# Margins on the estimated readiness of small products, and masked keys made one group ahead, in a two-layer decoder step

## The chip, the cores and the metric

The kernel runs on one core of a Trainium2 chip. The metric is the device time of one execution in microseconds (us). The core has five engines that the text names: PE (TensorE, the matrix products), DVE (VectorE), ACT (ScalarE), POOL (GpSimd) and SP (SyncE, which issues the DMA transfers). Each works through its own instructions in the order of the program and waits at an instruction until the data of the others are there.

## The reference

One inference step of a two-layer decoder of width 1024, for a prompt of 1024 tokens and for 8 samples of 4 new tokens each. Layer 0 is sliding-window attention with sinks, layer 1 is a gated DeltaNet. All data are float32. Cut to what matters:

```python
for layer in range(2):
    h = rms_norm(x, norm_g) * (1 + scale) + shift          # shift, scale, gate from silu(c) @ w_mod
    if layer == 0:                                         # 16 heads of 64, 4 kv heads, window 128
        q, k, v, z = split(h @ w_in)
        attn = sink_softmax(q k^T / 8, band) v             # samples: 128 cached keys and 4 new ones
        out = (attn * silu(z)) @ w_out
    else:                                                  # 8 key heads, 16 value heads of 128
        qkv, z, a, b = split(h @ w_in)
        q, k, v = silu(conv4(qkv))                         # depthwise, 4 taps; q, k normalized
        beta = sigmoid(b);  g = -exp(a_log) * softplus(a + dt_bias)
        for each chunk of 64 tokens:                       # w_v, w_k from a triangular solve
            u = w_v - w_k S
            o = (q e^gc) S + tril(q k^T decay) u
            S = S * e^(sum g) + (k e^(gtot - gc))^T u
        out = (rms_norm(o) * silu(z)) @ w_out
    x = x + gate * out
y = rms_norm(x, final_norm_g)
# outputs: y of prompt and samples, the new k/v caches, conv states and states S (8 x 16 x 128 x 128)
```

## The kernel before

**Products.** The large products are the four projections (in and out, of both layers). Each operand is split into a high and a low part of a shorter float format, and three products (high by high, high by low, low by high) are added up. In the profile they write `ps_pj`, `ps_tr` or `ps_ob` and read `hhi`/`hlo` or `h2hi`/`h2lo` with `wh`/`wl`; in the second out-projection the weights lie in `h2hi`, `h2lo`, `whB`, `wlB` and the moving side is `ohi`/`olo`. They depend on little and are the material with which PE is kept busy. Everything else on PE is small: transposes through the identity `cst`, products of single chunks or heads.

**How the order is made.** Each engine executes in program order, so the order in which the Python code emits instructions is all there is of a schedule. `Core` (L96 to L175) is a planner's clock: `issued` (L111) adds an estimated duration to `free[eng]` for each emitted instruction, from a table of rates (L130 to L144), and notes in `written` when each tile is ready. Every instruction passes the wrapper at L89, so nearly all rows of the profile say L89, and one goes by the names of tiles. The small steps are generators (the text calls them jobs) in a list sorted by rank (`weave` L485, ranks in `K` and `KR` at L241 and L242). After each large product `stages` (L496) goes through the list and lets each job run on while its condition is true. The conditions:

- `ready(*ts)` (L520): the tiles are estimated to be written by the time that PE's clock shows. It stands before a small product, so that the product is emitted when its operands should be there.
- `soon` (L523) and `idle` (L526): the same with 0.4 and 0.8 us of grace, before evacuations and work of other engines.
- `bank(tag)` and `give`: a PSUM bank of that tag (2 of `mi`, 2 of `lg`, 2 of `pj`, 1 of `tr`, 1 of `ob`).

Where no large product is to be had, `until` (L507) moves PE's clock on by 0.1 us and tries again; the emitted program then has no product in between, and PE really waits.

**The stages, in order of time** (from the trace). To 378 us the modulation and the projections and attention of layer 0. Then `cached` and `cached_pair` (L1034, L1067), the samples' attention: per pair of samples the keys `kc` are transposed, logits `ps_lg`, softmax into `sp` on DVE and ACT, `sp` transposed through `ps_mi` into `spT`, times the cached values `vc` into `ps_ob`. The z projection is the large work beside it. `gate_rows` (L423) then spreads the modulation over rows with a selection matrix `selt`. From 418 us the out-projection of layer 0, beside it `shape` (L1375), which scales and transposes blocks of the residual (`dg` is a diagonal of 1/rms) into the next layer's input.

From about 540 us layer 1. `decays` (L1501) makes the a/b projection `abT`, turns it into `AB`, from it the decays `g` and `gpr`, their running sum `gc` and the rows `gbs`; all that works with a chunk needs them. The heads go in eight pairs. For pair hq: `taps` (L1671) is the convolution on DVE from the projected rows `XR` into `qT`, `kT`, `vT` (`samples`, L1686, does it for the sample tokens, with the conv state `st`); `turn` in `proj_v` (L1734) transposes the values; `decay_blocks`, `solve`, `invert` and `blocks` make the triangular inverses (`X`, `UZ`, `us`, `DP`); `chain` (L1985) goes through the chunks in sequence with the state `S`, and `output` (L2031) is its product of queries, `uo` and state. The keys of pair r+1 are projected only when the chain of pair r-1 is finished (L2170).

From about 1455 us the out-projection of layer 1, `out_block` (L2312), with the samples beside it: `core` (L2424) makes their delta rule in sample layout (`KQT`, `qk`, `oH`; its `turned`, L2438, is a transpose of several tiles), and the block of the 32 sample rows waits for `core` (L2200). `new_states` (L2621) updates the 8 x 16 states: per group of two head pairs ACT masks the keys of one sample into `kb` (96 rows), per head pair PE multiplies `kb` by `U96` (`U` in the profile) into a bank of `mi`, and DVE adds two halves to the loaded state (`S1` in the code, `S` in the profile), which SP stores when its group of heads is full. The last steps are the final norm of the last block, `xt`, and its store.

## Time and profile before

| | |
|---|---|
| median of 3 runs | 1741.56 us (1740.1 to 1749.42) |
| the profiled execution | span 1740.3 us, 31813 instructions |
| busy: PE, DVE, ACT, POOL | 94%, 69%, 50%, 35% |
| busy of PE, 600 to 700 us and 700 to 800 us | 91.07 and 81.83 of 100 us |
| busy of PE, 1100 to 1200 us | 99.50 of 100 us |
| DMA, mean | 110 GB/s |

The profile comes from one execution. A row of the timeline has start, duration, engine, the line, the operation, the tile written and the tiles read, and in brackets the time that the engine stood idle before it and what ended that. A row of the waits has the engine with the tile it wrote, what it waited for, the sum in us, the number of waits and the longest. A row of a stretch has the stretch, its length, the busy time of PE, its weight loads, DVE, ACT and POOL (in brackets how many instructions), the granted clock of TensorE as a share of full speed, the DMA share and GB/s.

### The profile page before, as it was taken

The numbers are of one execution on the slowest core, as the hardware profiler recorded it, in microseconds if no ns is written. First come the engines' busy times: TensorE is split into PE (matmuls) and PEld (weight loads), VectorE is DVE, ScalarE is ACT, GpSimd is POOL, SyncE is SP. The second block draws the span as 40 slices with busy tenths as digits, with TensorE's granted clock in tenths as the row PEclk, the third lists the DMA queues.
The fourth block names the chain that finished last, engine by engine and source line by source line (L and its number), as shares of the span: only waits on it lengthen the run. The fifth ranks groups of instructions, "written<-read, shape, count | busy, mean of one in ns | idle before, by whom it ended". The sixth has DMA issues, their size and how long they took to land. (4 is left out here: it accounts for less than half of the span.)

```text
span 1740.3 us, 31813 instructions
## 1 busy us (share of the span) xinstructions
PE 1635.4 (94%) x10666; PEld 1436.2 (83%) x10666; DVE 1200.4 (69%) x3538; ACT 862.1 (50%) x2514; POOL 605.8 (35%) x1170
## 2 busy tenths in 40 slices
PE   6999999998999889789999999999999998989897
PEld 5988888986777789579999999899998996667685
DVE  4526775654565678876878789778788775367676
ACT  4625555543334555156554655654756654343332
POOL 2601111122122244344454544545345454333332
PEclk9999999999999999899999999999999999999998
DMA  9542121133233322222422323224232137854885
GB/s 328 154 130 73 50 62 53 48 99 107 89 133 91 88 65 63 61 66 68 117 58 75 96 57 105 70 76 111 52 112 61 45 91 223 232 180 153 252 251 163
DMA packets 281573, 191.77 MB, mean 110 GB/s; under 512 B 98362, under 2 KB 253882, under 8 KB 281379
## 3 DMA queue, kind: packets, MB, share of 16 engines
q1 hardware_dynamic: 281410, 189.75, 37.6%
q8 instruction: 84, 1.38, 0.3%
q14 instruction: 79, 0.64, 0.1%
HBM read 144.68 MB, written 47.04 MB: 110 GB/s over the span
## 5 line engine op out<-in xcount | busy, mean ns | idle before, releaser
L89 PE MATMUL ps_pj<-h2hi,wh 128*128 128x384 f32 (+1 forms) x1128 | 380.5, 337 | 2.1 <-ACT wh L89 2.1
L89 PE MATMUL ps_pj<-h2hi,wl 128*128 128x384 f32 (+1 forms) x1128 | 380.0, 337 | 0.7 <-POOL wl L89 0.7
L89 PE MATMUL ps_pj<-h2lo,wh 128*128 128x384 f32 (+1 forms) x1128 | 377.8, 335 | 0.0
L89 POOL TENSOR_TENSOR wl<-wr,wh 128x512 fp32r<-128x512 f32 x122 | 165.9, 1361 | 526.6 <-ACT wh L89 465.5
L89 PEld LDWEIGHTS ps_pj<-h2hi,wh 128*128 128x128 f32 x1128 | 214.1, 190 | 4.6 <-ACT wh L89 2.5
L89 PEld LDWEIGHTS ps_pj<-h2hi,wl 128*128 128x128 f32 x1128 | 214.2, 190 | 3.8 <-POOL wl L89 1.1
L89 PEld LDWEIGHTS ps_pj<-h2lo,wh 128*128 128x128 f32 x1128 | 213.9, 190 | 2.5
L89 POOL TENSOR_TENSOR xt<-xt,y 128x512 f32<-128x512 f32 (+1 forms) x48 | 64.0, 1338 | 173.8 <-DVE y L89 142.4
L89 DVE SCALAR_TENSOR_TENSOR vT<-XR,cT,vT 128x384 f32<-128x384 f32 (+1 forms) x144 | 95.3, 675 | 39.8 <-ACT vT L89 38.1
L89 PE MATMUL ps_pj<-hlo,wh 128*128 128x384 f32 (+1 forms) x360 | 119.0, 331 | 0.0
L89 PE MATMUL ps_pj<-hhi,wh 128*128 128x384 f32 (+1 forms) x360 | 118.4, 329 | 0.0
L89 PE MATMUL ps_pj<-hhi,wl 128*128 128x384 f32 (+1 forms) x360 | 117.9, 328 | 0.0
L89 DVE TENSOR_TENSOR tmp<-X 64x31 f32<-64x31 f32 (+15 forms) x248 | 93.7, 378 | 9.4 <-POOL X L89 5.9
L89 DVE TENSOR_TENSOR X<-X,tmp 64x31 f32<-64x31 f32 (+15 forms) x248 | 89.1, 359 | 8.5
L89 ACT CAST wh<-wr 128x512 fp32r<-128x512 f32 x122 | 75.2, 617 | 13.2 <-PE ps_pj L89 9.0
L89 PEld LDWEIGHTS ps_pj<-hlo,wh 128*128 128x128 f32 x360 | 67.7, 188 | 11.2 <-issue 11.1
L89 ACT ACTIVATE vo<-vo,fo 128x128 f32<-128x128 f32 x128 | 42.4, 392 | 61.5 <-POOL fo L89 61.5
L89 POOL TENSOR_TENSOR rst<-rsw 128x4 f32<-128x4 f32 x96 | 24.2, 252 | 131.8 <-DVE rsw L89 122.9
L89 PEld LDWEIGHTS ps_pj<-hhi,wh 128*128 128x128 f32 x360 | 67.7, 188 | 2.7 <-issue 2.7
L89 ACT COPY XR<-ps_pj 128x384 f32<-128x384 f32 (+1 forms) x96 | 43.0, 448 | 54.2 <-PE ps_pj L89 54.2
L89 ACT ACTIVATE prob<-prob,nm 128x256 f32<-128x256 f32 (+1 forms) x128 | 62.2, 489 | 14.8 <-DVE nm L89 14.6
L89 PEld LDWEIGHTS ps_pj<-hhi,wl 128*128 128x128 f32 x360 | 67.7, 188 | 2.1 <-issue 2.1
(580 smaller groups left out, 4262.0 us busy)
## 6 DMA issues: line engine op xcount, KB each, us to landing
wr<-in_gdn_w_in SPq DMA_DIRECT2D x96, 256.0 KB
S<-in_state_gdn_s SPq DMA_DIRECT2D x40, 256.0 KB
xt<-in_x_prompt SPq DMA_DIRECT2D x16, 512.0 KB
wm<-in_w_mod SPq DMA_DIRECT2D x16, 512.0 KB
wr<-in_swa_w_in SPq DMA_DIRECT2D x64, 128.0 KB
wmod<-in_w_mod SPq DMA_DIRECT2D x32, 256.0 KB
wm<-in_w_mod SPq DMA_DIRECT2D x32, 256.0 KB
DP<-gcr SPq DMA_DIRECT2D x64, 128.0 KB
```

The lines of the kernel that those rows point to most:

```text
L89: inst = fn(*args, **kwargs)
```

## The change

`ready` gets a margin, `lag`, in microseconds of the planner's clock: the product is emitted only when PE's clock is that much past the estimated readiness. At fifteen places a margin is given:

| place | tiles | margin |
|---|---|---|
| `gate_rows` L431 | `selt` | 2.5 |
| `cached_pair` L1079, L1112, L1122 | `kc`; `sp`; `pT` (`spT` in the profile) and `vc` | 1.5; 1.0; 1.0 |
| `shape` L1387 | `dg`, `xt` | 2.0 |
| `decays` L1536, L1583, L1590, L1621 | `abT`; `gp_` (`gpr`); `gc`; `gbs` | 1.5; 3.5; 1.0; 1.0 |
| `samples` L1687 | `st`, `XR` | 1.5 |
| `turn` L1736 | `u` (`vT` of the profile), `irk` | 1.0 |
| `output` L2035 | `S`, `uo` | 0.6 |
| `turned` L2438; for KQ L2544 | its sources (`qk`, `oH` and others); `KQT` | 1.0; 3.0 |
| `new_states` L2655 | `kb`, `U96`, `st` | 0.5 |

In `new_states` the mask `kb` of the next group is made behind the first product of a group, where before it was made in front of the product that reads it. There are two buffers of `kb` in both.

```diff
-    def ready(*ts):
-        return lambda: plain() or nc.ready(ts) <= nc.free["tensor"]
+    def ready(*ts, lag=0.0):
+        return lambda: plain() or nc.ready(ts) + lag <= nc.free["tensor"]
...
-        yield ready(gp_)
+        yield ready(gp_, lag=3.5)
...
+        def masked(g):
+            b, hq = g // 4, 2 * (g % 4)
+            kb = su.tile([96, 2, P], F32R, tag="kb", name="kb", bufs=2)
+            nc.scalar.activation(kb.rearrange("p h k -> p (h k)"), f(K96[:, hq * P:(hq + 2) * P]), AF.Copy,
+                                 scale=C["bsel"][0:96, b:b + 1])
+            return kb
+
+        g = 0
+        yield idle("scalar", K96)
+        ahead = masked(0)
         while units:
             fetch()
             b, h0, n, st = units.pop(0)
             for hh in range(n // 2):
                 hq = h0 // 2 + hh
                 if hh % 2 == 0:
-                    yield idle("scalar", K96)
-                    kb = su.tile([96, 2, P], F32R, tag="kb", name="kb", bufs=2)
-                    nc.scalar.activation(kb.rearrange("p h k -> p (h k)"), f(K96[:, hq * P:(hq + 2) * P]), AF.Copy,
-                                         scale=C["bsel"][0:96, b:b + 1])
-                yield ready(kb, U96, st)
+                    kb, g = ahead, g + 1
+                yield ready(kb, U96, st, lag=0.5)
                 pu = yield from bank("mi")
                 nc.tensor.matmul(pu[:, 0:256], kb[:, hh % 2, :], U96[:, 2 * hq * P:(2 * hq + 2) * P],
                                  start=True, stop=True)
+                if hh % 2 == 0 and g < 4 * DB:
+                    yield idle("scalar")
+                    ahead = masked(g)
```

No instruction is added or left out; the order moves on every engine from the samples' attention on, since each condition that comes true later moves all that follows it. Three places show it.

DVE in `decays`, between the a/b values and `gpr` (`pl` is a polynomial, `x` and `g` the decays; `qT` and `kT` are taps of the convolution of head pair 0, with the projected rows `XR`). Before:

```order
L89 SCALAR_TENSOR_TENSOR kT<-XR_5998,cT,kT 128x256
L89 SCALAR_TENSOR_TENSOR qT<-XR_5999,cT,qT 128x384
L89 SCALAR_TENSOR_TENSOR kT<-XR_5998,cT,kT 128x256
L89 SCALAR_TENSOR_TENSOR qT<-XR_5999,cT,qT 128x384
L89 SCALAR_TENSOR_TENSOR kT<-XR_5998,cT,kT 128x256
L89 SCALAR_TENSOR_TENSOR pl<-pl,s_6335 128x144 x7
L89 SCALAR_TENSOR_TENSOR pl<-pl,s 128x144
L89 SCALAR_TENSOR_TENSOR qT<-XR_5999,cT,qT 128x256
L89 TENSOR_SCALAR x<-x 128x144
L89 SCALAR_TENSOR_TENSOR x<-pl,x 128x144
L89 SCALAR_TENSOR_TENSOR g<-x,al 128x144
L89 COPY gpr<-g 128x128
```

and of the change:

```order
L89 TENSOR_SCALAR pl<-s_6363 128x144
L89 SCALAR_TENSOR_TENSOR kT<-XR_5943,cT,kT 128x256
L89 SCALAR_TENSOR_TENSOR pl<-pl,s_6363 128x144
L89 SCALAR_TENSOR_TENSOR kT<-XR_5943,cT,kT 128x256
L89 SCALAR_TENSOR_TENSOR pl<-pl,s_6363 128x144
L89 SCALAR_TENSOR_TENSOR kT<-XR_5943,cT,kT 128x256
L89 SCALAR_TENSOR_TENSOR pl<-pl,s_6363 128x144 x5
L89 SCALAR_TENSOR_TENSOR pl<-pl,s 128x144
L89 TENSOR_SCALAR x<-x 128x144
L89 SCALAR_TENSOR_TENSOR x<-pl,x 128x144
L89 SCALAR_TENSOR_TENSOR g<-x,al 128x144
L89 COPY gpr<-g 128x128
```

Before, four `qT` taps stand between `AB` and `gpr` (the first right in front of these rows); in the change none does, and the three `kT` taps stay.

PE in the second out-projection, at the transposes of `oH` in `core` and behind them. Before (the first `64x512` product, of the sample rows' block, comes 19 rows behind the first row):

```order
L89 MATMUL ps_lg<-cst,oH 128x128 x4
L89 MATMUL ps_mi<-U_17847,kb 128x256
L89 MATMUL ps_tr<-h2hi,ohi 128x512
L89 MATMUL ps_tr<-h2hi,olo 128x512
L89 MATMUL ps_tr<-h2lo,ohi 128x512
L89 MATMUL ps_ob<-h2hi,ohi 128x512
L89 MATMUL ps_ob<-h2hi,olo 128x512
L89 MATMUL ps_ob<-h2lo,ohi 128x512
L89 MATMUL ps_mi<-U_17847,kb 128x256
L89 MATMUL ps_ob<-h2hi,ohi 128x512
```

and of the change:

```order
L89 MATMUL ps_ob<-h2hi,ohi 128x512
L89 MATMUL ps_ob<-h2hi,olo 128x512
L89 MATMUL ps_ob<-h2lo,ohi 128x512
L89 MATMUL ps_lg<-cst,oH 128x128 x4
L89 MATMUL ps_mi<-U_17847,kb 128x256 x6
L89 MATMUL ps_pj<-h2hi,ohi 64x512
```

The out-projection's large products of this block have moved in front of `oH`; behind it stand six products of new states and then the sample block.

PE at the end of the program. Before:

```order
L89 MATMUL ps_ob<-h2lo,ohi 128x512
L89 MATMUL ps_ob<-h2hi,ohi 128x512
L89 MATMUL ps_ob<-h2hi,olo 128x512
L89 MATMUL ps_ob<-h2lo,ohi 128x512
L2712 UNCONDITIONAL_BRANCH
```

and of the change:

```order
L89 MATMUL ps_ob<-h2hi,ohi 128x512
L89 MATMUL ps_ob<-h2hi,olo 128x512
L89 MATMUL ps_ob<-h2lo,ohi 128x512
L89 MATMUL ps_mi<-U_17847,kb 128x256 x5
L2722 UNCONDITIONAL_BRANCH
```

Five products of new states, which before stood ahead of the last block, now stand behind the last product of the out-projection.

More of the change, by code (lines that the diff above doesn't have):

```diff
@@ L430, in gate_rows @@
         for j in range(2):
-            yield ready(selt)
+            yield ready(selt, lag=2.5)
             pg = yield from bank("lg")
@@ L1078, in cached_pair @@
             for r in range(2):
-                yield ready(kc)
+                yield ready(kc, lag=1.5)
                 pt = yield from bank("mi")
@@ L1111, in cached_pair @@
             nc.vector.tensor_scalar_mul(sp, sp, su)
-            yield ready(sp)
+            yield ready(sp, lag=1.0)
             pt = yield from bank("mi")
@@ L1121, in cached_pair @@
             give("mi", pt)
-            yield ready(pT, vc)
+            yield ready(pT, vc, lag=1.0)
             for kv in range(4):
@@ L1386, in shape @@
             for kk in range(2):
-                yield ready(dg, xt)
+                yield ready(dg, xt, lag=2.0)
                 pt = yield from bank("lg")
@@ L1535, in decays @@
             give("lg", pj)
-        yield ready(abT)
+        yield ready(abT, lag=1.5)
         pt = yield from bank("lg")
@@ L1589, in decays @@
         nc.vector.tensor_copy(gcf, pt[:, 0:P])
-        yield ready(gc)
+        yield ready(gc, lag=1.0)
         p2 = yield from bank("lg")
@@ L1620, in decays @@
         weave(decayed(0, states[0]), "decayed", 0)
-        yield ready(gbs)
+        yield ready(gbs, lag=1.0)
         pt = yield from bank("lg")
@@ L1686, in samples @@
                     def samples():
-                        yield ready(st, XR[:, TP:])
+                        yield ready(st, XR[:, TP:], lag=1.5)
                         pt = yield from bank("tr")
@@ L1735, in turn @@
                         yield lambda: "irk" in st
-                        yield ready(u, st["irk"])
+                        yield ready(u, st["irk"], lag=1.0)
                         pt = yield from bank("tr")
@@ L2034, in output @@
                 vt = vo[cp_]
-                yield ready(S, uo)
+                yield ready(S, uo, lag=0.6)
                 pb = psb("mi")
@@ L2436, in t2, with turned @@
             return sl.tile([P, DS, P], dt, tag="t2", name=nm, bufs=4)
-        def turned(dst, srcs, parts=P):
-            yield ready(*srcs)
+        def turned(dst, srcs, parts=P, lag=1.0):
+            yield ready(*srcs, lag=lag)
             pt = yield from bank("lg")
@@ L2544, in core @@
             yield from turned(lambda pt: nc.scalar.copy(KQ[:, (1 - i) * DS:(2 - i) * DS, :].rearrange("p t d -> p (t d)"), pt),
-                              [KQT[:, :, i, t] for t in range(DS)])
+                              [KQT[:, :, i, t] for t in range(DS)], lag=3.0)
         uH = VH
```

## The prediction

> **What bounds the kernel.** First the page, then the busy time by stretches of 100 us, for a full and a poor stretch.
>
> ```profile
> span 1740.3 us, 31813 instructions
> PE 1635.4 (94%) x10666; PEld 1436.2 (83%) x10666; DVE 1200.4 (69%) x3538; ACT 862.1 (50%) x2514; POOL 605.8 (35%) x1170
> ```
> ```profile
> 700.00:800.00 100.00, 81.83 (x600) 70.19 (x599) 76.22 (x215) 43.81 (x137) 34.97 (x99) 0.90 0.21 59
> 1100.00:1200.00 100.00, 99.50 (x705) 93.86 (x704) 79.33 (x230) 60.09 (x193) 45.27 (x115) 1.00 0.32 86
> ```
>
> TensorE (PE) is busy for 94% of the span. At 1100 us it has no time to give; at 700 us it is short by 18% and has a granted clock of 0.90. So time can only come from PE's waits and from the clock they cost. PE's waits, by what ended them (total, times, longest):
>
> ```profile
> PE ps_mi L89 <- ACT kb L89: 8.9, 3, 5.8
> PE ps_tr L89 <- ACT vT L89: 7.7, 3, 6.0
> PE ps_mi L89 <- ACT uo L89: 7.2, 4, 2.8
> PE ps_mi L89 <- DVE UZ L89: 6.6, 5, 2.1
> PE ps_lg L89 <- DVE KQT L89: 4.0, 1, 4.0
> PE ps_lg L89 <- DVE gpr L89: 3.2, 1, 3.2
> PE ps_tr L89 <- ACT XR L89: 2.6, 1, 2.6
> PE ps_lg L89 <- issue: 2.2, 1, 2.2
> PE ps_mi L89 <- DMA kc<-in_cache_swa_k: 2.2, 2, 1.1
> PE ps_lg L89 <- DVE dg L89: 2.0, 2, 1.7
> PE ps_ob L89 <- DVE spT L89: 1.4, 2, 0.8
> PE ps_mi L89 <- DVE sp L89: 1.2, 2, 0.6
> PE ps_tr L89 <- ACT vo L89: 2.4, 3, 1.4
> ```
>
> All but UZ and vo are places that get a margin: 8.9 + 7.7 + 7.2 + 4.0 + 3.2 + 2.6 + 2.2 + 2.2 + 2.0 + 1.4 + 1.2 = 42.6 us. Each is a small product at PE's head, in front of large products that were ready. A wait also costs clock: the last figure but two of each stretch is the granted clock, and around the one wait for XR a large product lengthens.
>
> ```profile
> 405.00:420.00 15.00, 10.78 (x111) 7.51 (x110) 5.70 (x27) 5.47 (x16) 0.00 (x0) 0.77 0.19 56
> 640.00:660.00 20.00, 13.95 (x83) 13.35 (x83) 14.43 (x32) 16.05 (x48) 7.83 (x13) 0.83 0.12 30
> 1555.00:1575.00 20.00, 15.96 (x68) 13.05 (x67) 18.33 (x45) 6.12 (x15) 7.38 (x5) 0.83 0.54 171
> 1615.00:1635.00 20.00, 14.19 (x54) 11.25 (x53) 10.84 (x25) 5.23 (x11) 4.92 (x4) 0.83 0.89 272
> ```
> ```profile
> 780.59 0.30 PE L89 MATMUL ps_tr<-cst,XR 128*35 128x128 f32 x1 [2.64 <-ACT XR L89]
> 781.08 0.34 PE L89 MATMUL ps_pj<-h2hi,wl 128*128 128x384 f32 x1
> 781.84 0.52 PE L89 MATMUL ps_pj<-h2hi,wl 128*128 128x384 f32 x1
> ```
>
> A clock of 0.83 over 20 us is 20 x 0.17 = 3.4 us of full-speed work lost. Behind a wait of only 2.64 us a product goes from 0.34 to 0.52 us. [...]
>
> **Part by part** (gains negative).
>
> *Cached attention, 378 to 420 us.* The margins of kc, sp and pT/vc eat their waits. But the last z products now stand one softmax earlier, and the last pair has none.
>
> ```profile
> 407.27 0.32 DVE L89 CUSTOM_DVE_ANT_0 sp<-ps_lg,smk 128x160 f32<-128x160 f32 x1
> ```
> ```profile
> 410.77 0.41 PE L89 MATMUL ps_mi<-cst,sp 128*128 128x128 f32 x2 [0.65 <-DVE sp L89]
> 415.38 1.19 PE L89 MATMUL ps_lg<-modG,selt 128*128 128x512 f32 x1 [2.21 <-issue]
> ```
>
> From the start of the last pair's softmax to the transpose of its weights it is 410.77 - 407.27 = 3.5 us; large products cover all of it but 0.65. Now only small ones stand there, of which I count two of 0.41, which leaves 2.7 bare, then 0.8 for spT. The selection (the product of 415.38; its wait is the row of 2.2 put down to issue) moves behind the first out-projection products, and its 2.2 goes over to these, whose operand comes out of the same last steps. Against 2.2 + 1.2 + 1.4 + 2.2 = 7.0 now, 2.7 + 0.8 + 2.2 = 5.7: **-1** (ends -7, nothing bare, and +3, if the bare stretch costs a further 3.4 of clock).
>
> *Shaping, dg.* A margin of 2.0 against waits of 1.7 and 0.3: **-1.5** (-2 to 0).
>
> *Decays, head pair 0 and its chain, 570 to 770 us.* On DVE four qT taps leave the path from AB to gpr.
>
> ```profile
> 577.36 0.62 DVE L89 SCALAR_TENSOR_TENSOR qT<-XR,cT,qT 128x384 f32<-128x384 f32 x1
> 578.30 0.64 DVE L89 SCALAR_TENSOR_TENSOR qT<-XR,cT,qT 128x384 f32<-128x384 f32 x1
> 579.26 1.65 DVE L89 SCALAR_TENSOR_TENSOR qT<-XR,cT,qT 128x384 f32<-128x384 f32 x1
> 584.00 1.48 DVE L89 SCALAR_TENSOR_TENSOR qT<-XR,cT,qT 128x256 f32<-128x256 f32 x1
> 586.37 0.23 DVE L89 COPY gpr<-g 128x128 f32<-128x128 f32 x1
> 648.02 0.62 DVE L89 SCALAR_TENSOR_TENSOR vT<-XR,cT,vT 128x384 f32<-128x384 f32 x1 [5.12 <-ACT vT L89]
> ```
> ```profile
> 641.53 0.23 ACT L89 ACTIVATE us<-us 128x32 f32<-128x32 f32 x1 [4.81 <-POOL us L89]
> ```
>
> They are 0.62 + 0.64 + 1.65 + 1.48 = 4.4 us, so gpr comes 4.4 earlier and PE's 3.2 there goes. Up to 641.53 ScalarE (ACT) waited 4.81 us for POOL's `us`, with four exponentials and vT queued behind it; PE waited 6.0 and DVE, inside the inverse of pair 0, 5.1. In the new order that `us` stands behind the exponentials. Both put chain 0 ahead by 4.4 + 5.1 = 9.5. What PE itself saves ahead of that counts no further: in the stretch from 700 us it has no large product left (pair 2's keys wait for chain 0) and stands for UZ, 6.6 us, without a margin. **-9.5** (ends -12.7, if gpr's 3.2 counts as well, and -3, if the margins of abT, gc, gbs and turn push the chain back).
>
> *XR at 778 us.* A margin of 1.5 against 2.6, and 1.5 for the products that went at 0.52 for 0.34 behind it, some eight: **-3** (-4.3, the whole wait and 1.7, to 0).
>
> *800 to 1450 us.* uo without its longest, 7.2 - 2.8 = 4.4, and vT without its longest, 1.7: 6.1 to be had; a margin of 0.6 on uo takes a part: **-4** (-6.1 to +3, as every unneeded margin also delays). *uo at 1500 us*, 0.6 of 2.8: **-1** (-2.8 to 0).
>
> *The samples' core, 1520 to 1600 us.* KQT's margin of 3.0 leaves 1.0 of the 4.0, so -3.0, and with so short a wait the clock's 3.4 goes. Against that, the large products that lay behind oH now lie ahead of it, and the last block's first product follows oH with six products of U96 and kb between. Each of these is followed by two updates of S on DVE:
>
> ```profile
> L89 DVE SCALAR_TENSOR_TENSOR S<-S,gtb,ps_mi x128: 328/342/351, 1588.3 to 1716.8; 128x128 f32<-128x128 f32 x128
> ```
>
> 6 x 2 x 0.342 = 4.1 us bare, which also covers the samples' path from oH to their operand. -3.0 - 3.4 + 4.1 = **-2.5** (-7.4 to +1).
>
> *New states, 1588 to 1740 us.* The mask kb stands in ACT's queue behind casts that wait for data.
>
> ```profile
> 1620.31 0.62 ACT L89 CAST h2hi<-wr 128x512 fp32r<-128x512 f32 x1 [3.62 <-DMA wr<-in_gdn_w_out]
> 1624.79 0.62 ACT L89 CAST ohi<-of 128x512 fp32r<-128x512 f32 x1 [3.86 <-DMA of<-gTd]
> 1625.32 0.90 ACT L89 ACTIVATE kb<-K,cst 96x256 fp32r<-96x256 f32 x2
> ```
>
> A group ahead, kb is done before these. [...] Of PE's 5.8, about 2 stays, because its next large products need h2hi's cast of 1620.31 and the low part made from it. 5.8 - 2.0 = 3.8, the other kb waits 8.9 - 5.8 = 3.1, and half of the clock's 3.4: 8.6, of which I take **-8** (-12.3 to -2, if h2hi holds PE all the same).
>
> *The end.* Now PE's last kb product is at 1714.67 and the last output leaves SP at 1736.74, behind y's scaling alone.
>
> ```profile
> 1714.67 0.41 PE L89 MATMUL ps_mi<-U,kb 96*128 96x256 f32 x1
> ```
> ```profile
> 1736.74 0.81 SPq L89 DMA_DIRECT2D out_y_p<-xt  x2
> ```
>
> In the new order the last five of them follow the last out-projection product, with their updates of S between and behind the steps of y, and one more store of S behind out_y_p on SP. Two pairs of updates ahead of y's first step, one between, one behind: 4 x 2 x 0.342 = 2.7, and 0.8 of SP's time: **+3.5** (0, if DVE's gaps there take them, to +8, if the store's landing is bare).
>
> *Fresh waits.* From 378 us on, most rows have moved against each other. Where no margin helps, such a wait is 0.8 us (vo: 2.4 in 3); ten of them, an estimate, **+8** (+4 to +12).
>
> Sum: -1 - 1.5 - 9.5 - 3 - 4 - 1 - 2.5 - 8 + 3.5 + 8 = **-19**. The profiled execution, span 1740.3, is 1.3 below the runs' median of 1741.56; it becomes 1721.3, the median **1722.5**. The margins add no instruction.
>
> **Rivals.**
>
> *All waits go.* If the bare stretches above are covered, 42.6 us of waits and the clock of the four stretches, 3 x 3.4 + 15 x 0.23 = 13.7, less the end's 3.5, go: 1741.56 - 52.8 = 1689. For it: nearly each margin is about as long as its wait. Against it: pair 0's chain and the core are latencies that no product shortens. 0.10.
>
> *The wait is only renamed.* The margin is counted on the planner's clock; it gives one rate for taps that took 0.62 and 1.65 us. Then the chain's part is -3, kb's -5, dg and uo keep -1.5 and -1, XR -1, the rest nothing, with +3.5 and +8: +0, so 1741.5. For it: UZ, 6.6 us, has no margin and ends the stretch of 700 us. 0.22.
>
> *Slower: the cover is used up.* Each margin spends large products earlier than before, and where a stage ends none are left. That costs +3 in the cached stage; 4.1 and half of a clock's 3.4 before the last block, together 5.8; 8 at the end; and gpr, gc and gbs, behind their margins, make chain 0 no earlier. kb's -8, KQT's -3, dg's -1.5 and uo's -1 stay, 13.5, and the fresh +8; the rest is nothing: 3 + 5.8 + 8 - 13.5 + 8 = +11.3, so 1753. That is 30.3 worse than my sum (4 cached, 9.5 chain, 3 XR, 4 steady, 5.3 core, 4.5 end); it decides from 27.7 on, the 19 and the 8.7 below. For it: PE's new order has no large product before the last block and behind the last out-projection. Against it: PE is 99.5% busy from 1100 us, so large products are plenty in most stages. 0.12.
>
> **Numbers.** My forecast keeps 0.56. 0.5% is 8.7 us, about what a measurement of this kernel can tell from no change: faster is below 1732.9, slower above 1750.3. Faster: 0.56 + 0.10 = 0.66; same 0.22; slower 0.12. The half-widths of the terms (5, 0.8, 4.9, 2.2, 4.6, 1.4, 4.2, 5.2, 4, 4), taken as independent, make 12.4 (root of the sum of squares), so the forecast's own range is 1710 to 1735. Up to the rename and past it, and down towards the first rival, 1699 to 1747 leaves out the slower case and most of the first rival, 0.2.
>
> **What would show it.** Right: no kb wait above 2.5 us, no vT wait of 6, gpr's copy 4 us sooner behind AB, the end of the stretch with UZ waits 9 us earlier, a clock near 1 around KQT, and fresh waits in the last pair of the cached stage, before the 64-row block and at the end. Wrong: chain 0 starting as late as before, or over 12 us between the last out-projection product and the end.

## The result and the profile after

| | before | the change |
|---|---|---|
| median of the timed runs | 1743.24 us (10 runs, 1738.19 to 1749.42) | 1754.5 us (10 runs, 1750.36 to 1762.17) |
| ratio to before, 95% interval | 1 | 1.0065 [1.0048, 1.0082] |
| span of the profiled execution | 1740.3 us | 1756.5 us |

The change makes the kernel 0.65% slower. Forecast were 1722.5 us, with a range of 1699 to 1747. The page of the profile after, its first line and the engines' busy time:

```profile
span 1756.5 us, 31785 instructions
PE 1645.5 (94%) x10666; PEld 1442.6 (82%) x10666; DVE 1213.7 (69%) x3538; ACT 866.2 (49%) x2514; POOL 608.0 (35%) x1170
```

The share of PE is the same, and so is the number of instructions of each engine. With the same 10666 products PE is busy 1645.5 - 1635.4 = 10.1 us longer, and it stands 1756.5 - 1645.5 = 111.0 us instead of 104.9. Its waits after the change, by what ended them (total, times, longest):

```profile
PE ps_mi L89 <- DVE us L89: 16.5, 14, 2.9
PE ps_mi L89 <- DVE S L89: 12.2, 11, 3.1
...
PE ps_mi L89 <- ACT KT L89: 3.9, 1, 3.9
PE ps_lg L89 <- POOL AB L89: 3.4, 1, 3.4
...
PE ps_pj L89 <- DVE y L89: 2.9, 1, 2.9
...
PE ps_lg L89 <- DVE KQT L89: 1.6, 1, 1.6
...
PE ps_mi L89 <- ACT kb L89: 1.5, 1, 1.5
...
PE ps_tr L89 <- ACT vT L89: 1.4, 2, 0.9
...
PE ps_mi L89 <- ACT uo L89: 0.3, 1, 0.3
```

Against the same rows before, most margins did what they say: kb went from 8.9 to 1.5, vT from 7.7 to 1.4, uo from 7.2 to 0.3, KQT from 4.0 to 1.6, and gpr and XR are gone. The eleven rows that the prediction adds up to 42.6 us come to 8.5 (the four just named, dg with 1.1, spT with 1.7 and sp with 0.9). But others took their place, against which no margin was set. KT, AB and y are new, and us and S stood in before with

```profile
PE ps_mi L89 <- DVE us L89: 6.9, 8, 1.5
...
PE ps_mi L89 <- DVE S L89: 2.4, 6, 0.6
```

Since PE stands 6.1 us more in all, the other waits grew by 34.1 + 6.1 = 40.2 us.

**Where the time came.** A tally from the traces says where a kernel falls behind. In each trace the 5992 large products are numbered in order of their start. The start of the nth, minus its start in the kernel before, is how far the kernel is behind there (both counted from the 100th product). Columns are named by the time of that product before the change; the last is the time from the last large product's start to the end of the span, 10.5 us before.

| kernel (change against before) | 481 | 557 | 692 | 894 | 1484 | 1640 | 1730 | end |
|---|---|---|---|---|---|---|---|---|
| the change | +3.7 | +7.3 | +5.4 | -0.3 | +16.6 | +17.1 | +10.4 | 15.7 |
| e1 margins, old masks | +3.8 | +9.7 | +8.0 | +1.7 | +16.7 | +14.4 | +8.4 | 20.3 |
| e2 masks ahead alone | -0.2 | +0.1 | 0.0 | +1.2 | +4.6 | +3.8 | +0.7 | 11.1 |
| e3 margins selt to gbs | +2.9 | +6.5 | +7.0 | +5.9 | +16.4 | +14.1 | +9.6 | 12.6 |
| e4 margins from XR on, masks | -0.6 | -1.9 | -1.4 | -6.8 | +2.9 | +8.0 | +1.3 | 15.5 |
| e5 the change without kc, dg | +0.2 | +2.9 | -3.3 | -8.8 | +7.0 | +7.5 | +0.7 | 15.5 |
| e6 kc alone | +5.2 | +5.3 | +2.6 | +3.0 | +7.5 | +6.6 | +3.6 | 11.3 |
| e8 0.1 at all | -7.3 | -7.2 | -10.7 | -14.5 | -13.2 | -13.1 | -11.9 | 15.4 |
| e9 e5 without uo | -0.8 | -0.7 | -6.7 | +1.5 | +2.3 | +6.1 | -0.6 | 15.5 |
| e10 e5 without XR, vT, uo | -0.9 | -0.8 | -4.7 | -3.1 | +2.7 | +10.6 | +3.9 | 15.5 |
| e11 e5 with a margin on us | -1.2 | -1.0 | -7.3 | +4.4 | +31.5 | +31.7 | +24.9 | 15.5 |
| e12 core and kb, masks | -0.9 | -2.4 | -3.7 | -2.0 | +5.7 | +4.1 | -1.1 | 14.8 |
| e13 0.25 at all | -8.1 | -6.2 | -10.4 | -8.6 | +5.1 | +0.7 | -2.0 | 13.7 |
| e14 0.4 at all | -4.6 | -1.4 | -6.9 | +3.6 | +14.5 | +18.0 | +12.7 | 15.1 |
| e15 e5 without kb's margin | +0.2 | +0.3 | -6.1 | -12.2 | +2.2 | +8.2 | +1.4 | 10.7 |
| e16 0.1 at all, masks ahead | -8.7 | -8.7 | -11.5 | -16.0 | -15.8 | -18.4 | -24.5 | 13.0 |
| e17 dg alone | +1.6 | +7.3 | +12.2 | +13.4 | +15.9 | +13.1 | +12.9 | 11.0 |
| e18 uo alone | +2.6 | +1.2 | -0.5 | -3.5 | -1.4 | -2.4 | -2.1 | 11.9 |

How far such a number can be trusted shows in kernels whose order is still that of before: e2 and e12 up to some 1520 us, e18 up to some 740 us, e4 up to some 576 us. At 481 and 557 us these stand between -2.4 and +2.6, and from 894 to 1484 us e12 falls 7.7 us behind with the order unchanged. So one trace tells a loss of some 3 us in the first stages and of 8 us further on, or a smaller one that several kernels with the same order repeat. Of the change's 16.2 us of span, 3.7 arise before 481 us, 3.6 up to 557, 16.9 between 894 and 1484, and 5.1 behind the last large product; 557 to 894 give 7.6 back and 1484 to 1730 give 6.2; 0.6 lie ahead of the 100th product, in an order that is the same.

### The profile page after: what moved, and what is told of

Its sections match the earlier page's. It is cut to its first block, busy times and chain, and to the rows that moved or that the text cites. A ratio compares the mean times of both kernels' runs of the same rounds, so it can differ in the third digit from the quotient of the medians.

```text
span 1756.5 us, 31785 instructions
## 1 busy us (share of the span) xinstructions
PE 1645.5 (94%) x10666; PEld 1442.6 (82%) x10666; DVE 1213.7 (69%) x3538; ACT 866.2 (49%) x2514; POOL 608.0 (35%) x1170
## 5 line engine op out<-in xcount | busy, mean ns | idle before, releaser
L89 DVE TENSOR_TENSOR X<-X,tmp 64x31 f32<-64x31 f32 (+15 forms) x248 | 97.8, 394 | 8.5
L89 ACT ACTIVATE qe<-ps_mi,Eg 128x128 f32<-128x128 f32 x112 | 35.1, 365 | 77.4 <-PE ps_mi L89 77.3
L89 ACT ACTIVATE prob<-prob,nm 128x256 f32<-128x256 f32 (+1 forms) x128 | 62.2, 489 | 14.8 <-DVE nm L89 14.6
```

The costliest lines, as they stand in the source:

```text
L89: inst = fn(*args, **kwargs)
```

## The experiments

Each kernel was timed against the kernel before on the same chip. Ratios are to before, with their 95% interval.

### Halves of the change: e1 to e4

e1 leaves out the second half of the diff:

```diff
-                    kb, g = ahead, g + 1
+                    yield idle("scalar", K96)
+                    kb = su.tile([96, 2, P], F32R, tag="kb", name="kb", bufs=2)
...
-                    ahead = masked(g)
```

> All fifteen margins, the masks kb made as before the change; up to about 1580 us the same order as the changed kernel. Theory A (the margins move rows so that others arrive late: heads of ACT's and DVE's queues, PSUM banks and unmargined products): slow already without the new masks, 1750 to 1762 us, and behind the same large product as in the changed kernel by about 15 us at 1430 us. Theory B (the new masks, whose S updates PE waits for at the end, make the loss): near the kernel before plus the 4 us of the attention stage, 1740 to 1748.

Measured: 1757.24 us, 1.0076 [1.0047, 1.0104]. The masks are not the loss; theory B falls. Between the change and e1 nothing is resolved.

e2 has that half and no margin:

```diff
-                yield ready(kb, U96, st, lag=0.5)
+                yield ready(kb, U96, st)
```

> No margin anywhere, only the masks kb one group ahead; the same order as the kernel before up to about 1580 us. Theory A: no loss, the kb waits of 8.9 us go and new ones come at S: 1733 to 1743 us. Theory B: the loss shows here, 1748 to 1756, with waits for S of 8 us or more and a longer end.

Measured: 1741.03 us, 0.9983 [0.9962, 1.0004]: no loss, and a gain that is not resolved. From 1640 to 1730 us it makes up 3.1 us.

e3 keeps the margins of selt, kc, sp, pT and vc, dg, abT, gpr, gc and gbs; for the others, as here:

```diff
-                yield ready(S, uo, lag=0.6)
+                yield ready(S, uo)
```

> Only the margins of selt, kc, sp, pT and vc, dg, abT, gpr, gc, gbs; none from the sample taps on, masks as before. Theory A: the first stages lose as in the changed kernel (4 us at 418 us, 4 to 5 more by 575), the chain of pair 0 gives back about 6 by 700, and behind that the scatter of a moved order: 1740 to 1755. Theory C (only the margins inside the pairs, of turn and of uo, push the chains and make the loss between 900 and 1450 us): no loss in 900 to 1450, 1738 to 1745.

Measured: 1757.82 us, 1.0082 [1.0058, 1.0107], above the range of either theory. These margins alone make the whole loss. The chain of pair 0 gave nothing back here, where 6 us were expected. From 894 to 1484 us it loses 10.5 us with no margin inside the pairs, so theory C, that only the margins inside the pairs make that loss, doesn't hold as put.

e4 is the complement, for example:

```diff
-            yield ready(selt, lag=2.5)
+            yield ready(selt)
```

> Only the margins from the sample taps on (samples, turn, uo, turned, KQT, kb) and the masks ahead; the order of before up to about 580 us. Theory A: the waits for vT, uo, XR, KQT and kb go, others come at us, UZ and S: 1738 to 1758, a loss in 900 to 1450 us of another size and at other places than in the changed kernel. Theory C: the same loss in 900 to 1450 us as in the changed kernel, about 13 us, so 1750 to 1756.

Measured: 1751.91 us, 1.0051 [1.003, 1.0072], which theories A and C both allow; from 894 to 1484 us it loses 9.7. The profiled executions of e3 and e4 took 1753.48 and 1747.1 us, 4.3 and 4.8 below their medians, so that the times weigh more here than the tally. Two halves with a loss of 0.8% and 0.5%, and a whole with 0.65%: they don't add up.

### Single places: e5, e6, e17

e5 is the change without two margins:

```diff
-                yield ready(kc, lag=1.5)
+                yield ready(kc)
...
-                yield ready(dg, xt, lag=2.0)
+                yield ready(dg, xt)
```

> The changed kernel without the margins of kc and dg; all others and the early masks stay. If the margin of kc makes the loss of the attention stage (the copy of KT then stands behind a cast that waits for its weights) and that of dg the one at 541 us: level with the kernel before at 480 us within 2 us (the changed kernel is 3.7 behind) and no more than 4 behind at 560 us (it is 7.3). Theory A (any moved order brings other waits) expects that this is not kept to the end: 1744 to 1758 us. Theory D (those two places are the loss) expects 1738 to 1746.

Measured: 1743.57 us, 1.0007 [0.9991, 1.0024]: the whole loss is gone with two of fifteen margins. It doesn't follow that these two make it in every order: e4 above and e9 and e10 below have neither, and are 0.40 to 0.62% slower than before.

e6 has kc's margin alone:

```diff
-                yield ready(kc)
+                yield ready(kc, lag=1.5)
```

> The kernel before with one margin alone, 1.5 for kc. If kc's margin makes the loss of the attention stage: 2 to 4 us behind at 480 us. What follows has no margin, but another order. Theory A: a further gain or loss of up to 10 us between 550 and 1740 us at places without margin, 1740 to 1756. Theory D: the 2 to 4 us stay as they are, 1744 to 1748.

Measured: 1745.51 us, 1.0017 [0.9995, 1.004], not resolved as a time. In the tally it is 5.2 behind at 481 us. The three kernels with kc's margin among others are 2.9 to 3.8 behind there, the five without it and with the other early margins (e5, e9, e10, e11, e15) -1.2 to +0.2, and the highest of all kernels without it is e18 with +2.6. So kc's margin costs some 3 to 5 us in that stage. How, the rows show. Before, ACT's copy of the transposed keys KT:

```profile
384.00 1.06 ACT L89 COPY KT<-ps_mi 64x512 f32<-64x512 f32 x2
```

and after the change, ACT, then PE:

```profile
390.18 0.62 ACT L89 CAST whi<-wor 128x512 fp32r<-128x512 f32 x1 [4.17 <-DMA wor<-in_swa_w_out]
390.71 0.57 ACT L89 COPY KT<-ps_mi 64x512 f32<-64x512 f32 x1
```
```profile
391.33 1.06 PE L89 MATMUL ps_mi<-cst,kc 128*64 128x128 f32 x4 [3.87 <-ACT KT L89]
392.52 0.52 PE L89 MATMUL ps_pj<-hhi,wl 128*128 128x384 f32 x1
```

The transposes of kc come later, so the copy that empties their bank comes later in ACT's order, and now stands behind a cast that waits 4.17 us for its weights. PE's next transposes need that bank and wait 3.87 us, more than the two waits of 1.1 us for kc that the margin was to remove. The large product behind them takes 0.52 us. The other kernels repeat it: with kc's margin PE waits at this place for KT for 3.8 (e1), 2.5 (e3) and 4.3 us (e6), each time behind such a cast, which waits 3.5 to 4.9 us; in the kernels without it, no wait for KT there exceeds 0.6 us.

e17 has dg's margin alone:

```diff
-                yield ready(dg, xt)
+                yield ready(dg, xt, lag=2.0)
```

> The kernel before with one margin alone, 2.0 for dg in the shaping. If it alone makes the loss at 540 to 580 us: AB on DVE starts 8 us or more later than before (572.5 us), a large product waits about 2.8 us for a PSUM bank near 560 us, and the kernel is 3 to 6 us behind at 557 us; time 1744 to 1756. If the loss needs kc's margin too: AB within 3 us of before, 1738 to 1746.

Measured: 1750.48 us, 1.0044 [1.0017, 1.007]; the profiled execution 1752.8 us, 12.5 above that of before. At 557 us it is 7.3 us behind, more than the 3 to 6 expected, and 14.5 at 595 us (the 1900th large product), which it never makes up. Here is DVE's copy of the a/b values, the head of pair 0's chain, and that of gpr, in before (whose gpr stands in the prediction), e17, the change, and e10, which has neither kc's nor dg's margin:

```profile
572.54 0.51 DVE L89 COPY AB<-ps_lg 128x256 f32<-128x256 f32 x2 [3.06 <-PE ps_lg L89]
```
```profile
586.34 0.51 DVE L89 COPY AB<-ps_lg 128x256 f32<-128x256 f32 x2 [3.41 <-PE ps_lg L89]
596.46 0.23 DVE L89 COPY gpr<-g 128x128 f32<-128x128 f32 x1
```
```profile
587.98 0.51 DVE L89 COPY AB<-ps_lg 128x256 f32<-128x256 f32 x2 [3.69 <-PE ps_lg L89]
598.09 0.23 DVE L89 COPY gpr<-g 128x128 f32<-128x128 f32 x1
```
```profile
572.48 0.51 DVE L89 COPY AB<-ps_lg 128x256 f32<-128x256 f32 x2 [1.29 <-PE ps_lg L89]
582.96 0.23 DVE L89 COPY gpr<-g 128x128 f32<-128x128 f32 x1
```

AB comes 13.8 us later with dg's margin alone, 15.4 in the change (0.6 of it from before the 100th product), and as before without it. By the tally the transposes of abT stand behind 1807 large products in e17 and 1800 in before, so hardly any large product moved in front of them. From 535 us to these transposes PE is busy 32.29 of 35.29 us in before and 38.54 of 49.09 in e17. So it stands 7.6 us longer; the other 6.2 of the 13.8 are longer busy time, with more transposes and a lower clock (0.91 for 0.95 from 535 to 600 us). PE's longest waits in this stretch of e17:

```profile
539.13 1.13 PE L89 MATMUL ps_lg<-dg,xt 128*128 128x128 f32 x8 [2.12 <-POOL XR L89]
542.15 0.58 PE L89 MATMUL ps_lg<-h2hi,wab 128*64 128x384 f32 x1 [1.90 <-POOL wab L89]
...
566.50 0.44 PE L89 MATMUL ps_pj<-h2hi,wh 128*128 128x384 f32 x1 [2.84 <-DVE y L89]
...
571.97 2.05 PE L89 MATMUL ps_lg<-dg,xt 128*128 128x128 f32 x8 [2.42 <-DVE dg L89]
```

with the stretch from 535 to 600 us as a whole in before and in e17 (PE's busy time, and the clock as the last figure but two):

```profile
535.00:600.00 65.00, 58.37 (x349) 53.73 (x348) 35.77 (x93) 32.90 (x78) 17.13 (x30) 0.95 0.28 78
```
```profile
535.00:600.00 65.00, 51.68 (x295) 45.70 (x293) 38.74 (x102) 30.09 (x64) 16.01 (x23) 0.91 0.21 63
```

The reason is in the code of `project`: the large products of layer 1 wait for the shaping itself, in `until(lambda: shaped[0] >= (4, 7, 9)[gi])`. A margin on dg puts off the shaped blocks, and with them the products that were to cover it. Before, three products with kw0h stand in front of the dg that PE waits for at 539 us; in e17 none does (1707 and 1704 large products ahead of it). There is nothing to emit, the planner moves its clock on, and PE waits. That the rule in `project` is the link is read from code and order; it was not tried by itself.

### Opposite sign, and a margin for all: e7, e8, e13, e14

e7 has every margin with a minus:

```diff
-            yield ready(selt, lag=2.5)
+            yield ready(selt, lag=-2.5)
```

> All margins with the opposite sign: the fifteen places are issued earlier than estimated, by the same sizes; masks as before. The waits at these places (44 us before) must grow, by up to the margins. Theory A in its strong form (the kernel before has an order picked out of many, and any other order of the same code costs about 0.5%, whatever its sense): 1750 to 1765, the waits at the fifteen places longer and partly given back by fewer waits at us, UZ and S. Theory E (later issue is wrong in sense, and margins cost because they delay what follows): faster than before, 1725 to 1740.

Measured: 1820.72 us, 1.0458 [1.0423, 1.0492]. Its waits:

```profile
PE ps_tr L89 <- ACT vT L89: 25.2, 27, 4.8
...
PE ps_lg L89 <- DVE oH L89: 10.0, 1, 10.0
```

It is slower than theory A expected, and theory E is wrong outright. Issue before the estimate costs far more than the other moved orders: vT's waits go from 7.7 to 25.2 us. That these places lose by being issued earlier doesn't show that they gain by being issued later.

e8, e13 and e14 give every small product the same margin, 0.1, 0.25 and 0.4 us:

```diff
-        return lambda: plain() or nc.ready(ts) <= nc.free["tensor"]
+        return lambda: plain() or nc.ready(ts) + 0.1 <= nc.free["tensor"]
```

> The kernel before with a margin of 0.1 us at every small product: too small to remove a wait of 1 us or more, but it moves the order. Theory A, strong form: 1745 to 1758 us, with new waits at places of no connection. Theory E or D: 1740 to 1746, no change that can be measured.

Measured: 1732.69 us, 0.9942 [0.9921, 0.9963], faster, as no theory had it.

> The kernel before with a margin of 0.25 us at every small product. Theory G (later issue pays in itself, since the planner's estimate of readiness is too early by some tenths): no worse than with 0.1, 1722 to 1734 us, and fewer waits of PE in all. Theory A (a moved order scatters by some 0.5% to either side, and 0.1 was a lucky one): anywhere in 1730 to 1760, with no tie to the dose.

Measured: 1743.11 us, 1.0027 [1.0007, 1.0048].

> The kernel before with a margin of 0.4 us at every small product. Theory G: within 0.5% of the 0.25 us, either side, and below 1740, unless the chains of the head pairs, in which each step then waits 0.4 us, end later: then waits in the stretch of 700 us grow and 1745 or more. Theory A: 1730 to 1760 at random.

Measured: 1758.63 us, 1.0115 [1.0093, 1.0137]. The stretch from 692 us on loses in e14, as theory G allowed for 0.4; but 0.25 is slower than 0.1 by 0.9%, where G had it no worse. So a general margin doesn't pay by its dose, and theory A, in the form that any other order is worse, fell with e8. What is left is that the time goes with the order, in a way that none of these theories foretold: without e7, the other orders tried here lie between 1.1% faster (e16) and 1.75% slower (e11).

### Inside the pairs: e9, e10, e11, e18

e9 is e5 without uo's margin:

```diff
-                yield ready(S, uo, lag=0.6)
+                yield ready(S, uo)
```

> The changed kernel without the margins of kc, dg and uo. Ahead of the kernel before by 8 to 9 us at 890 us, as with kc and dg alone taken out. Theory F (the margin of 0.6 on uo turns its waits into waits for us and UZ, which end in the same chains, and into slow-clock stretches, 10 to 16 us between 890 and 1490 us): uo waits of 6 us come back, waits for us fall from about 10 to 4 us, the loss in 890 to 1490 is under 6 us, and the time 1730 to 1738. Theory A (scatter of a moved order): a loss there of anything from 0 to 16 us with no tie to uo, 1732 to 1752.

Measured: 1747.09 us, 1.004 [1.0019, 1.0061]. Between 894 and 1484 us the loss falls from 15.8 (e5) to 0.8 us and the waits for us from 10.2 to 2.7, as theory F had it, though uo's waits are 2.1 and not 6. But between 692 and 894 us it now loses 8.2 where e5 gains 5.5, and the time is outside F's range and worse than e5's.

e10 leaves out the margins of the sample taps and of turn as well:

```diff
-                        yield ready(st, XR[:, TP:], lag=1.5)
+                        yield ready(st, XR[:, TP:])
...
-                        yield ready(u, st["irk"], lag=1.0)
+                        yield ready(u, st["irk"])
```

> The changed kernel without the margins of kc, dg, uo, u (turn) and the sample taps; those of selt, sp, pT, abT, gpr, gc, gbs, the core, KQT and kb stay, and the masks ahead. Theory F: as with uo alone taken out, 1728 to 1738, with vT and XR waits back. If the margins of u and the sample taps make the loss: better than with uo alone taken out by 4 us or more. Theory A: 1732 to 1752 at random.

Measured: 1749.85 us, 1.0062 [1.0038, 1.0087]: without the margins inside the pairs the kernel is 0.5% slower than e5 with them. Theory F's time was wrong.

e11 is e5 with a margin more:

```diff
-                yield ready(us)
+                yield ready(us, lag=0.6)
```

> The changed kernel without the margins of kc and dg, and with one margin more, 0.6 for the product of us in the chains. If a margin at the place that waits now is all that lacks: the waits for us fall from 10 to under 4 us and the loss in 890 to 1490 with them, 1732 to 1740. Theory F (the chains are a latency and a margin only hands its wait on to the next product): the waits come back at S, UZ or vo, 1740 to 1755.

Measured: 1770.37 us, 1.0175 [1.0158, 1.0192]. Waits for us fall between 890 and 1490 us from 10.2 to 5.9, S grows from 1.2 to 5.6, and from 894 to 1484 us the kernel falls behind by 27.1 us, e5 by 15.8. On this step of the chain the margin only delayed the chain.

e18 is before with uo's margin alone:

```diff
-                yield ready(S, uo)
+                yield ready(S, uo, lag=0.6)
```

> The kernel before with one margin alone, 0.6 for uo. If the margin only renames: between 890 and 1490 us the uo waits fall from 7 to under 2 us, those for us rise from 2 to 8 or more, the sum of PE's waits there stays at 16 us or grows, and the time is 1738 to 1750. If it works as meant: the sum falls by 4 us or more, 1732 to 1738.

Measured: 1739.17 us, 0.9971 [0.9947, 0.9995]. PE's waits between 890 and 1490 us, first in before, then in the change, then in e18:

```profile
PE ps_mi L89 <- ACT uo L89: 7.2, 4, 2.8
...
PE ps_mi L89 <- DVE us L89: 1.8, 3, 1.1
...
PE ps_tr L89 <- ACT vT L89: 1.2, 1, 1.2
```
```profile
PE ps_mi L89 <- DVE us L89: 11.0, 8, 2.9
PE ps_lg L89 <- DVE UZ L89: 5.0, 3, 2.5
```
```profile
PE ps_tr L89 <- ACT vT L89: 3.4, 6, 1.7
PE ps_tr L89 <- ACT XR L89: 3.0, 2, 2.3
PE ps_mi L89 <- DVE us L89: 2.4, 4, 0.9
PE ps_mi L89 <- ACT uo L89: 2.4, 1, 2.4
```

uo's margin removes 4.8 us of its waits, and us stays near what it was, so the wait is not handed on to us, as theory F had it. But the sum doesn't fall either: all rows of that stretch come to 16.1 us in before and 17.4 in e18, with vT up to 3.4 and XR, which had no wait there before, at 3.0. Neither branch of the expectation came as put, and that the margin is worth the measured 0.3% isn't shown by the waits. The change has 23.9 there; e2 and e12, in before's order, have 19.1 and 21.5.

Set side by side, long waits for us come where uo's margin stands together with the others inside the pairs. The five kernels with the margins of the sample taps, turn and uo and no other margin in the chains (the change, e1, e4, e5, e15) wait 9.7 to 11.8 us for us between 890 and 1490 us, and fall 9.7 to 16.9 us behind from 894 to 1484. e9, which is e5 without uo's, waits 2.7 and loses 0.8. e3, with none of the three, waits 1.5 and loses 10.5 all the same, so these waits are not the whole of the loss there.

### The end: e12, e15

e12 leaves out all margins ahead of the core:

```diff
-            yield ready(gp_, lag=3.5)
+            yield ready(gp_)
```

> The kernel before up to about 1520 us; only the margins of the core (1.0, KQT 3.0) and of kb (0.5), and the masks ahead. The KQT wait of 4 us and the kb waits go; against that the bare stretch before the sample rows' block (4 us), waits for S and five or six products of new states behind the last out-projection, 3 to 6 us more behind the last large product. Sum by these: 0 to +5 us, 1742 to 1748. If the margin of kb has no such price: 1732 to 1738.

Measured: 1741.26 us, 1.001 [0.9994, 1.0025]. From 1484 to 1730 us it gains 6.8, and 4.3 are lost at the end. e15 is e5 without kb's margin:

```diff
-                yield ready(kb, U96, st, lag=0.5)
+                yield ready(kb, U96, st)
```

> The changed kernel without the margins of kc, dg and kb (the other margins and the masks ahead stay). If kb's margin puts the last products of new states behind the last out-projection product and makes the longer end: none stands there, 10 to 11 us from the last large product to the end as before the change, not 15, and 3 to 5 us less than with kc and dg alone taken out: 1737 to 1741. If the end is as long for another reason: 1742 to 1746.

Measured: 1742.44 us, 1.0011 [0.9992, 1.0031]. The end is 10.7 us, near the 10.5 before the change, and no product of new states stands behind the last out-projection product: kb's margin does make the longer end, 15.5 us in e5. The time is e5's all the same: in this order 14.0 us are lost between 1590 and 1640 us, where e5 loses 7.3, and the place and the price don't add up again.

### The fastest: e16

e16 is e8 with the masks ahead:

```diff
-        return lambda: plain() or nc.ready(ts) + lag <= nc.free["tensor"]
+        return lambda: plain() or nc.ready(ts) + 0.1 <= nc.free["tensor"]
```

> 0.1 us at every small product, and the masks one group ahead, no other margin. If the masks ahead are worth what they gave alone (0.2%, 3 us) on top of the 0.1: 1727 to 1732 us. Theory A: the gain behind 1580 us is another in another order, 1728 to 1740.

Measured: 1719.45 us, 0.9888 [0.9866, 0.9909], faster than both kernels and below both ranges expected. From 1640 to 1730 us it gains 6.1 us; the masks alone (e2) gained 3.1 there, the 0.1 alone lost 1.2. Of its other gains, 8.7 us come up to 481 us, all in the samples' attention (at 370 us it is 2.5 behind), and 7.3 between 557 and 894. The stretch of 378 to 418 us in before, the change and e16 (PE's busy time is the first figure behind the length):

```profile
378.00:418.00 40.00, 32.93 (x376) 27.61 (x375) 18.59 (x58) 15.92 (x41) 7.59 (x9) 0.93 0.45 132
```
```profile
378.00:418.00 40.00, 33.03 (x376) 28.88 (x375) 14.96 (x49) 14.39 (x38) 7.08 (x9) 0.91 0.40 118
```
```profile
378.00:418.00 40.00, 39.86 (x381) 34.74 (x370) 21.38 (x59) 17.40 (x44) 9.98 (x11) 1.00 0.42 119
```

In e16 z products last to the end of the stage, and PE hardly stands there. The 0.1 alone (e8) does this too, with 40.00 us busy. Which of the many moved products brings that was not taken apart.

## Why the prediction was wrong

Two steps of the prediction failed. One is the sentence on which the gains rest, that each waiting product stands "in front of large products that were ready": behind dg there were none, and behind kc the wait came back at another place. The other is a term of the sum, the fresh waits. I put them at +8; the waits at the margins' places fell by 34.1 us, and the others grew by 40.2, beside 10.1 us by which PE's busy time grew. Traces with one order differ among themselves by up to 5.4 us of waits in one stretch (16.1 in before, 21.5 in e12), which is too little to account for that.

**Cached attention, -1.** Measured +3.7. The last pair was not the trouble: from 400 to 425 us PE waits 0.9 us for sp, 1.7 for spT and 0.7 for the out-projection's operand, 3.3 in all where I had 5.7. The loss is the step "the margins of kc ... eat their waits": kc's didn't. I looked at which large products stand behind the transposes, and not at what the later copy is queued behind on ACT. That ACT's queue holds up what stands behind a waiting cast (kb at 1625.32, behind ohi's cast with its wait of 3.86 us) I had used for kb alone.

**Shaping, -1.5 with an end at 0.** This step failed most: 3.6 us up to 557 us, and AB 15.4 us late. dg alone makes the kernel 0.44% slower (e17). I took "a margin of 2.0 against waits of 1.7 and 0.3" as if there were products to put in front; these wait for dg's own result. No end of my range held a loss. (The half-width 0.8 in my list should be 1.0 by that range, which moves nothing.)

**Decays and chain 0, -9.5.** The path from AB to gpr got shorter as forecast: 598.09 - 587.98 = 10.1 us after the change, 13.8 before, 3.7 of the 4.4. But the margins of `decays` can't be credited with it: e17, which has none of them, takes 596.46 - 586.34 = 10.1 as well. And ACT's wait for `us` is gone:

```profile
653.01 0.23 ACT L89 ACTIVATE us<-us 128x32 f32<-128x32 f32 x1 [0.17 <-POOL us L89]
```

What this is worth in time isn't settled. Without kc's and dg's margins, e5, e9, e10 and e15 are 3.9 to 6.4 us better at 692 than at 557 us. At 894 us e5 and e15 are 11.7 and 12.5 better, e10 only 2.3, and e9 is 2.2 worse. The change is 1.9 better at 692, since its chain started late. XR's waits (-3) went.

**800 to 1450 us, -4 - 1.** Measured +16.9 from 894 to 1484 us in the change and 15.8 in e5, where two kernels with before's order (e2, e12) show +3.4 and +7.7. So a loss of some 8 to 13 us is left beyond that scatter. The sign of my -4 was wrong there. From 890 to 1490 us PE waits 23.9 us instead of 16.1, most of it at places without a margin, and its clock is 0.98 for 0.99, which by these rounded figures is some 6 us more (an estimate). The waits for us come with uo's margin and the others inside the pairs together; uo's alone doesn't bring them (e18). What makes the whole loss is open: e3 has 10.5 us of it without these margins, and in e9 it moves to the stage before.

**Core and new states, -2.5 - 8.** From 1484 to 1730 us the change gains 6.2, where I had 10.5; e12 gains 6.8, e2 3.9. The bare stretch behind oH is there, in the change:

```profile
1617.61 0.63 PE L89 MATMUL ps_lg<-cst,oH 128*128 128x128 f32 x4 [1.71 <-DVE oH L89]
...
1619.84 1.07 PE L89 MATMUL ps_mi<-U,kb 96*128 96x256 f32 x2 [1.36 <-DVE S L89]
1621.47 1.07 PE L89 MATMUL ps_mi<-U,kb 96*128 96x256 f32 x2 [0.56 <-DVE S L89]
1623.72 0.69 PE L89 MATMUL ps_pj<-h2hi,ohi 128*64 128x512 f32 x1 [1.18 <-DVE ohi L89]
```

From the last of the oH products to the first product of the block it is 1623.72 - 1618.24 = 5.5 us, of which three waits make 3.1. The clock around KQT is 1.00 now (1575 to 1595 us, with KQT's product at 1585.74 behind a wait of 1.57 us), as the sum has it. But from 1615 to 1635 us, where the bare stretch lies, it is 0.74, which is 20 x 0.26 = 5.2 us of full-speed work, and my sum counted no clock for that stretch.

**The end, +3.5.** Measured +5.1, for the reason given: the updates of S stand between y's steps.

```profile
1744.97 0.35 PE L89 MATMUL ps_mi<-U,kb 96*128 96x256 f32 x1 [3.09 <-DVE S L89]
...
1747.34 0.55 PE L89 MATMUL ps_mi<-U,kb 96*128 96x256 f32 x1 [1.49 <-DVE S L89]
```
```profile
1750.82 0.82 SPq L89 DMA_DIRECT2D out_y_p<-xt  x2
1751.73 0.40 SPq L89 DMA_DIRECT2D out_new_s_s<-S  x1
```

**The rivals.** The slower one gave 1753 us and a chance of 0.12, and the time is near it, but its reason holds in part only: the ends of the core and of the program are bare as it said. The larger losses, the bank behind ACT's cast and the products that wait for dg, it didn't name, so that its nearness is in part luck. That the waits are only renamed is right for the waits (34.1 us went, 40.2 came); it missed the 10.1 us of PE's busy time.

**The signs.** Of those for being right, kb's longest wait (1.5), vT's (0.9), gpr's copy 3.7 us sooner behind AB and the clock around KQT came; the stretch with the UZ waits didn't end 9 us earlier (0.3 ahead at 894 us). Both signs of being wrong came too: gpr, which chain 0 needs, comes at 598.09 instead of 586.37, and from the start of the last out-projection product to the end it is 15.7 us, more than the 12 set as a limit.

What is shown: dg's margin alone costs 0.44% (e17); kc's costs some 3 to 5 us in its stage and how (four kernels with it); kb's margin makes the longer end (e15); without kc's and dg's the loss is gone in one order (e5). What stays open: the 8 to 13 us inside the pairs, and why losses of single margins don't add up (e3, e4, e9, e10, e15). The orders tried here, e7 aside, lie from 1.1% faster to 1.75% slower, and this is of the size of everything that the margins were to gain.

## What to carry to other kernels

A margin on a step needs work to put in front of it, and this work must not wait for that step: look in the code at what the covering products wait for before pricing it at nothing. A product issued later also moves its evacuation back in the other engines' queues, so look there for a head that waits for data (here KT's copy, behind a cast that waited 4.17 us). Time such margins one by one, and hold each against a small neutral margin everywhere. Here 0.1 us everywhere with the masks ahead gained 1.1%, more than any margin timed alone (kc, dg, uo). But 0.25 and 0.4 us everywhere lost 0.3 and 1.15%, so that this is one good order found by trying, and no rule.

## What the runs showed of the hardware

In the change at 539 us, a step of DVE on one column took 0.16 us, and the two behind it, begun while POOL was splitting a weight, took 1.19. On DVE:

```profile
539.49 0.16 DVE L89 SCALAR_TENSOR_TENSOR rsw<-rst,rsw 128x1 f32<-128x1 f32 x1
539.68 1.19 DVE L89 TENSOR_TENSOR rst<-rsw 128x1 f32<-128x1 f32 x1
540.91 1.19 DVE L89 SCALAR_TENSOR_TENSOR rst<-rst,sv 128x1 f32<-128x1 f32 x1
```

and on POOL:

```profile
539.57 1.29 POOL L89 TENSOR_TENSOR kw0l<-wr,kw0h 128x512 fp32r<-128x512 f32 x1 [1.66 <-ACT kw0h L89]
540.81 1.27 POOL L89 TENSOR_TENSOR kw1l<-wr,kw1h 128x512 fp32r<-128x512 f32 x1
```

Each stretched step ends within 0.02 us of POOL's split of a weight (539.68 + 1.19 = 540.87 and 539.57 + 1.29 = 540.86; 540.91 + 1.19 = 542.10 and 540.81 + 1.27 = 542.08); the step of 539.49, which began before POOL's, kept its 0.16. That the split holds the step up is read from these times; by what means isn't shown. These are the steps ahead of dg, so each of these two splits delayed dg by 1.19 - 0.16 = 1.03 us here.
